# Low parts of the down-projection weights: a negated copy on ScalarE and an adding transfer instead of a subtraction on VectorE

## The chip, the cores and the metric

The kernel runs on one core of a Trainium2 chip. The metric is the device time of one execution in microseconds (us); of several runs the median is given.

## What is computed

A decoder trunk of two layers on an input of 512 tokens by 1024 columns in float32. Layer 0 mixes the tokens with gated linear recurrences, layer 1 with sparse attention. Each layer ends with a gated feed-forward block (FFN) with 2816 hidden columns, and that is the part that matters here:

```
def swiglu(h, w_gate_up, w_down):
    g, u = jnp.split(h @ w_gate_up, 2, axis=-1)
    return (jax.nn.silu(g) * u) @ w_down

h = h + swiglu(rmsnorm(h, ffn_norm[layer]), ffn_w_gate_up[layer], ffn_w_down[layer])
```

## The kernel before

Every matrix is used as a sum of two parts in the reduced format float32r: a high part (`wh` for weights) and a low part (`wl`, the weight minus its high part). A product of two such matrices is three matmuls: high by high, high by low, low by high (`mm3`, L86 to L90).

For a weight block, `load` (L58) has SP issue a transfer from memory into one of three buffers named `raw`. `split` (L70) then makes the two parts in pieces of 512 columns: ScalarE casts `raw` to `wh` (L77), VectorE subtracts `wh` from `raw` into `wl` (L78). `wh` and `wl` have seven buffers each. A `raw` buffer is free for the next load when all that read it is done.

The FFN (`ffn`, L270) goes over the hidden columns in 22 slices of 128, j = 0 to 21, in groups of 2, 4, 4, 4, 4, 4. In a slice:

- `weight_side` (L245) loads two blocks of gate and up weights of 512 KB each (L251), and makes from their quarters four sums on POOL (L259, L260, L262, L264). Each sum and three of the quarters are split into parts (`cut`, L208, and `split`). The sums let seven products stand for eight.
- Seven products (L290 to L299, called from L326 to L339) of 256 columns run on PE. ACT copies intermediate results (L327, L330, L335), VectorE adds (L331, L336, L338), POOL scales by the row norm (L341, L342), ACT applies the Silu (L343), VectorE multiplies (L344), and the result is split into `hh` (ACT, L347) and `hl` (VectorE, L348).
- From the second group on, each slice also multiplies two blocks of the second weight matrix with the hidden slices of the group before (`down`, L304 to L313, called at L352). Its weights come from `weight` (L66), 128x256 for the first group and 128x512 for the later ones.

After the last slice `down` runs once more in layer 0, for the eight blocks of the last group; in layer 1 `finish` (L363) does this instead, and gets its weights from `weight` as well.

The order of the instructions on each engine is set when the program is built, by a scheduler that works on the dependences; the engines then run their own lists in order. All transfers into `raw` are issued by SP, in order too.

Of the kernel before, what the change touches and what calls it, by code (L numbers as in the profile page):

```python
# [9 lines left out]
F32 = mybir.dt.float32  # L10
F32R = mybir.dt.float32r
U8 = mybir.dt.uint8
AF = mybir.ActivationFunctionType
ALU = mybir.AluOpType
# [3 lines left out]
P = 128  # L18
# [8 lines left out]
WS = 512  # L27
# [24 lines left out]
class Core:  # L52
# [17 lines left out]
    def split(self, raw, n, pool):  # L70
        nc = self.nc
        out = []
        for o in range(0, n, WS):
            m = min(WS, n - o)
            wh = self.wp.tile([P, WS], F32R, tag="wh", name="wh", bufs=7)
            wl = self.wp.tile([P, WS], F32R, tag="wl", name="wl", bufs=7)
            nc.scalar.copy(wh[:, :m], raw[:, o:o + m])  # L77
            (nc.gpsimd if pool else nc.vector).tensor_tensor(wl[:, :m], raw[:, o:o + m], wh.bitcast(F32)[:, :m],  # L78
                                                             ALU.subtract)
            out.append((wh, wl))  # L80
        return out

# [187 lines left out]
    def ffn(self, outs, w_out, gain, layer, next_gain):  # L270
        tc, nc, io, sp = self.tc, self.nc, self.io, self.sp
        with tc.tile_pool(name="fs", bufs=1) as fs, tc.tile_pool(name="fps", bufs=6, space=PSUM) as fps:
# [4 lines left out]
            for m in range(KD):  # L277
                ps = self.bank(self.turn + 1 + m // 3, "ps_o") if m in BANK_OUT else \
# [23 lines left out]
            out = []  # L302

            def down(hid, first, ms, last):  # L304

                nonlocal acc
                for m in ms:
                    ps = fps.tile([P, T], F32, tag="gu", name="ps_d") if last and m in OWN_DOWN else self.bank(m, "ps_d")
                    self.dense_t(ps, self.weight(io["dn"][layer, m, :, P * first:P * (first + len(hid))]), hid)
                    if last:  # L310
                        out.append(self.residual(m, ps, next_gain, acc))
                    else:
                        nc.vector.tensor_tensor(self.h[m], ps, self.h[m], ALU.add)  # L313


            before, first, done = None, 0, 0
            for size in GROUPS:
                hid = []
                for j in range(done, done + size):
# [30 lines left out]
                    if before:  # L350
                        n = KD // size
                        down(before, first, range((j - done) * n, (j - done + 1) * n), False)  # L352
                before, first = hid, done
                done += size
            tc.keep_in_program_order(nc.scalar.preload_act_table_set("natural_log_exp_and_others"))
            if next_gain is None:
                self.finish(hid, [io["dn"][layer, m, :, P * first:] for m in range(KD)], fps)
                return None, None
            acc = sp.tile([P, T], F32, tag="acc", name="acc", bufs=1)
            down(hid, first, range(KD), True)  # L360
            return out, acc

# [798 lines left out]
```

## Time and profile before

| | |
|---|---|
| median of 3 runs | 1341.58 us (1338.67 to 1341.74) |
| the profiled execution, its own time | 1340.35 us |
| its span, first to last instruction | 1338.2 us |
| mean granted TensorE clock | 0.98 |
| FFN of layer 0, POOL's first sum of the first and of the last slice | 272.3 and 602.3 us |
| FFN of layer 1, the same | 931.4 and 1261.5 us |

The profile is of one execution; its busy times are shares of the span. PE is TensorE, DVE VectorE, ACT ScalarE, POOL GpSimd, SP the engine that issues transfers (SPq its queue). A row of the timeline has the start, the duration, the engine and line, the operation with output and inputs, and in brackets how long the engine was idle before it and what released it.

### The profile page before, as it was taken

The page shows a single profiled execution, that of the slowest core. Times are in us where ns is not written, and L with a number is a line of the kernel's source. Part 1 is how long each engine was busy: PE and PEld are TensorE (multiplying, and loading weights), DVE is VectorE, ACT ScalarE, POOL GpSimd, SP SyncE. Part 2 cuts the span into 40 slices and gives each one's busy share as a digit, 9 for nine tenths or more (in the row PEclk, how much of TensorE's full clock was granted, in tenths as well). Part 3 has the DMA queues.
Part 4 walks back from the last instruction along what each step waited for, and adds up shares of the span by engine and source line. Part 5 has one row for each costly group of instructions (what it writes and reads, how often), then busy time and mean ns, then how long its engine had stood idle before and what let it go on. Part 6 is the DMA issues. An engine that isn't in the chain of part 4 may idle for free.

```text
span 1338.2 us, 21839 instructions
## 1 busy us (share of the span) xinstructions
PE 1276.7 (95%) x7846; PEld 1119.7 (84%) x7846; DVE 1016.4 (76%) x1829; ACT 729.4 (55%) x1587; POOL 643.9 (48%) x569
## 2 busy tenths in 40 slices
PE   9999999978999999999988999999799999999995
PEld 7888888868899888989876888877698999988883
DVE  7896764799999677775762888986989987766664
ACT  6655454655544444444554788995654444444444
POOL 3432430165666555553025666764665655555501
PEclk9999999999999999999998999999889999999997
DMA  7222211222233223332322211101123322223321
GB/s 254 84 74 69 79 49 63 79 83 79 84 103 110 95 96 99 107 102 89 104 86 94 72 56 48 48 9 63 51 84 124 98 96 95 95 95 96 103 63 63
DMA packets 44125, 115.13 MB, mean 86 GB/s; under 512 B 4913, under 2 KB 10481, under 8 KB 44017
## 3 DMA queue, kind: packets, MB, share of 16 engines
q1 hardware_dynamic: 43872, 113.69, 26.6%
q8 instruction: 62, 1.02, 0.3%
q14 instruction: 47, 0.38, 0.1%
q10 hardware_dynamic: 144, 0.04, 0.0%
HBM read 111.62 MB, written 2.10 MB: 85 GB/s over the span
## 4 chain that ended last, share of the span: by engine, by line
PE 54%; POOL 15%; DVE 15%; ACT 6%; DMA 6%; issue 5%; POOLq 0%; DVEq 0%; SPq 0%; ACTq 0%
DMA raw<-in_gu 5%; PE p L88 4%; PE p L89 4%; PE p L90 4%; PE ps_e L88 3%; PE ps_e L89 3%; PE ps_e L90 3%; DVE wl L78 3%; POOL sw L262 3%; POOL sw L264 3%; PE ps_d L90 3%; PE ps_d L89 3%; PE ps_d L88 3%; POOL sw L259 3%; POOL sw L260 2%
## 5 line engine op out<-in xcount | busy, mean ns | idle before, releaser
L78 DVE TENSOR_TENSOR wl<-raw,wh 128x512 fp32r<-128x512 f32 (+2 forms) x340 | 285.7, 846 | 51.1 <-ACT wh L77 50.4
L77 ACT CAST wh<-raw 128x512 fp32r<-128x512 f32 (+2 forms) x356 | 211.1, 604 | 179.9 <-PE p L89 44.9
L214 DVE TENSOR_TENSOR sl<-sw,sh 128x512 fp32r<-128x512 f32 x176 | 188.7, 1076 | 19.9 <-ACT sh L213 18.7
L259 POOL TENSOR_TENSOR sw<-raw 128x512 f32<-128x512 f32 x44 | 77.4, 1758 | 238.8 <-DMA raw<-in_gu 187.7
L213 ACT CAST sh<-sw 128x512 fp32r<-128x512 f32 x176 | 108.7, 617 | 118.0 <-PE p L89 80.9
L89 PE MATMUL ps_d<-hl,wh 128*128 128x512 f32 x344 | 136.1, 396 | 0.1
L90 PE MATMUL ps_d<-hh,wl 128*128 128x512 f32 x344 | 135.6, 394 | 0.0
L88 PE MATMUL ps_d<-hh,wh 128*128 128x512 f32 x344 | 135.0, 396 | 0.0
L343 ACT ACTIVATE g<-g 128x512 f32<-128x512 f32 x44 | 27.8, 632 | 135.7 <-POOL g L342 135.4
L344 DVE TENSOR_TENSOR g<-s,g 128x512 f32<-128x512 f32 x44 | 31.8, 722 | 72.1 <-ACT g L343 71.0
L927 POOL TENSOR_SCALAR p<-p,sm 128x128 f32<-128x128 f32 (+3 forms) x128 | 68.7, 557 | 32.5 <-DVE sm L924 11.9
L89 PE MATMUL ps_e<-xl,wh 128*128 128x512 f32 x192 | 76.8, 401 | 0.6 <-DVE xl L108 0.6
L88 PE MATMUL ps_e<-xh,wh 128*128 128x512 f32 x192 | 76.9, 404 | 0.2
L90 PEld LDWEIGHTS ps_d<-hh,wl 128*128 128x128 f32 x344 | 64.5, 188 | 14.8
L90 PE MATMUL ps_e<-xh,wl 128*128 128x512 f32 x192 | 76.5, 400 | 0.0
L918 ACT ACTIVATE p<-p,mx 128x256 f32<-128x256 f32 (+3 forms) x128 | 71.7, 565 | 8.8 <-DVE mx L910 8.3
L264 POOL TENSOR_TENSOR sw<-raw,sw 128x512 f32<-128x512 f32 x44 | 73.0, 1660 | 6.4 <-DVE sl L214 6.4
L89 PEld LDWEIGHTS ps_d<-hl,wh 128*128 128x128 f32 x344 | 64.7, 188 | 13.1 <-DVE hl L348 1.0
L88 PEld LDWEIGHTS ps_d<-hh,wh 128*128 128x128 f32 x344 | 64.5, 188 | 13.0
L262 POOL TENSOR_TENSOR sw<-raw 128x512 f32<-128x512 f32 x44 | 75.0, 1706 | 0.0
L342 POOL TENSOR_TENSOR g<-g,rstd 128x512 f32<-128x512 f32 x42 | 59.8, 1423 | 23.1 <-DVE g L338 23.1
L260 POOL TENSOR_TENSOR sw<-sw,raw 128x512 f32<-128x512 f32 x44 | 65.4, 1487 | 8.6 <-issue 4.8
(345 smaller groups left out, 4249.6 us busy)
## 6 DMA issues: line engine op xcount, KB each, us to landing
raw<-in_gu SPq DMA_DIRECT2D x88, 512.0 KB, 3.7
raw<-in_dn SPq DMA_DIRECT2D x80, 256.0 KB, 2.8
raw<-in_ein SPq DMA_DIRECT2D x22, 512.0 KB, 3.7
raw<-in_oin SPq DMA_DIRECT2D x12, 512.0 KB, 3.7
raw<-in_eout SPq DMA_DIRECT2D x8, 512.0 KB, 3.7
bias<-in_bias SPq DMA_DIRECT2D x16, 256.0 KB, 2.6
raw<-in_oout SPq DMA_DIRECT2D x8, 512.0 KB, 3.5
h<-in_x SPq DMA_DIRECT2D x8, 256.0 KB, 5.4
```

The costliest lines, as they stand in the source:

```text
L77: nc.scalar.copy(wh[:, :m], raw[:, o:o + m])
L78: (nc.gpsimd if pool else nc.vector).tensor_tensor(wl[:, :m], raw[:, o:o + m], wh.bitcast(F32)[:, :m], ALU.subtract)
L88: mm(ps, ah, bh, start=start, stop=False, skip_group_check=more)
L89: mm(ps, ah, bl, start=False, stop=False, skip_group_check=more)
L90: return mm(ps, al, bh, start=False, stop=stop, skip_group_check=more)
L213: nc.scalar.copy(hi, src)
L214: nc.vector.tensor_tensor(lo, src, hi.bitcast(F32), ALU.subtract)
L259: nc.gpsimd.tensor_tensor(s1, a21, a22, ALU.add)
L260: nc.gpsimd.tensor_tensor(s2, s1, a11, ALU.subtract)
L262: nc.gpsimd.tensor_tensor(s3, a11, a21, ALU.subtract)
L264: nc.gpsimd.tensor_tensor(s4, a12, s2, ALU.subtract)
L918: nc.scalar.activation(p, p, AF.Exp, bias=h["mx"][:, t, b:b + 1], scale=-1.0, accum_out=h["sm"][:, t, b:b + 1])
```

## The change

The weights of `down` come from a new method, `weight_add`, instead of `weight`. It casts as before, then ScalarE writes minus `wh` into `wl`, and a transfer issued by POOL adds `raw` onto `wl` inside SBUF. `finish` and all other weights keep `weight`.

```
@@ -77,6 +77,22 @@
+    def weight_add(self, ap):
+
+        nc = self.nc
+        n = ap.shape[1]
+        raw = self.load(ap)
+        out = []
+        for o in range(0, n, WS):
+            m = min(WS, n - o)
+            wh = self.wp.tile([P, WS], F32R, tag="wh", name="wh", bufs=7)
+            wl = self.wp.tile([P, WS], F32R, tag="wl", name="wl", bufs=7)
+            nc.scalar.copy(wh[:, :m], raw[:, o:o + m])
+            nc.scalar.activation(wl[:, :m], wh.bitcast(F32)[:, :m], AF.Identity, scale=-1.0)
+            nc.gpsimd.dma_start(wl.bitcast(F32)[:, :m], raw[:, o:o + m], accum_op=ALU.add)
+            out.append((wh, wl))
+        return out
...
@@ -306,7 +322,7 @@
-                    self.dense_t(ps, self.weight(io["dn"][layer, m, :, P * first:P * (first + len(hid))]), hid)
+                    self.dense_t(ps, self.weight_add(io["dn"][layer, m, :, P * first:P * (first + len(hid))]), hid)
```

Lines behind L81 stand 16 further down in the changed kernel: L259 becomes L275, L341 L357, L342 L358, L343 L359, L347 L363.

The order on the engines moves with it. On POOL, one slice in the late part of an FFN (the four sums, the scaling of `s` and of `g`). Before:

```order
L262 TENSOR_TENSOR sw<-raw 128x512
L341 TENSOR_TENSOR s<-s,rstd 128x256
L264 TENSOR_TENSOR sw<-raw,sw 128x512
L342 TENSOR_TENSOR g<-g,rstd 128x512
L259 TENSOR_TENSOR sw<-raw 128x512
L260 TENSOR_TENSOR sw<-sw,raw 128x512
```

And now:

```order
L278 TENSOR_TENSOR sw<-raw 128x512
L280 TENSOR_TENSOR sw<-raw,sw 128x512
L358 TENSOR_TENSOR g<-g,rstd 128x512
L95 DMA wl<-raw 128x512 x2
L275 TENSOR_TENSOR sw<-raw 128x512
L357 TENSOR_TENSOR s<-s,rstd 128x256
L276 TENSOR_TENSOR sw<-sw,raw 128x512
```

The two adds of a slice stand behind its last sum and the scaling of `g`, and ahead of the next slice's first sum.

On ACT, from the Silu of a slice to the casts of its two `dn` blocks. Before:

```order
L343 ACTIVATE g<-g 128x512
L213 CAST sh<-sw 128x512
L330 COPY u<-p_5607 128x256
L347 CAST hh<-g 128x512
L77 CAST wh<-raw 128x512 x2
L213 CAST sh<-sw 128x512
```

And now:

```order
L359 ACTIVATE g<-g 128x512
L93 CAST wh<-raw 128x512
L94 ACTIVATE wl<-wh 128x512
L363 CAST hh<-g 128x512
L93 CAST wh<-raw 128x512
L94 ACTIVATE wl<-wh 128x512
L229 CAST sh<-sw 128x512
```

The cast and the negation of the first block now stand directly behind the Silu, those of the second behind `hh`.

On SP, one slice of the changed kernel, with the semaphores that each issue waits for (DMAHW are those of SP's transfers, DMASW those of POOL's; 6 is the one that the add from `raw_5358` signals, 5 and 7 those of the second block's adds of the slice before and of this one):

```order
L63 DMA raw_5358<-in_dn 128x512 [waits DMAHW7_49,DMASW5_49,Activation_49]
L63 DMA raw_5379<-in_dn 128x512 [waits DMAHW0_49,DVE_49,Pool_49]
L267 DMA raw_5399<-in_gu 128x1024 [waits DMAHW1_49,DVE_49]
L267 DMA raw_5401<-in_gu 128x1024 [waits DMAHW2_49,DMASW6_49,Activation_49]
L63 DMA raw_5547<-in_dn 128x512 [waits DMAHW3_49,DMASW7_49,Activation_49]
```

The sequence of the loads is the one of before. The second gate/up block (`raw_5401`) waited for DVE there and now waits for the add from the first `dn` block.

## Rows read from the trace of the kernel before

**Rows 1.** The page: busy us, share of the span, instructions, by engine.

```profile
PE 1276.7 (95%) x7846; PEld 1119.7 (84%) x7846; DVE 1016.4 (76%) x1829; ACT 729.4 (55%) x1587; POOL 643.9 (48%) x569
```

**Rows 2.** Windows: length, busy PE, PEld, DVE, ACT, POOL, clock, DMA share, GB/s.

```profile
288.00:300.00 12.00, 4.79 (x35) 4.34 (x34) 12.00 (x20) 7.09 (x16) 5.96 (x4) 0.83 0.38 132
300.00:350.00 50.00, 45.99 (x339) 43.43 (x338) 48.38 (x69) 28.62 (x59) 31.54 (x19) 0.97 0.25 80
1099.98:1261.48 161.50, 159.48 (x1083) 144.90 (x1083) 115.89 (x171) 73.12 (x141) 86.92 (x61) 1.00 0.31 99
```

**Rows 3.** Timeline of POOL, one late slice in layer 1, next one's start.

```profile
1148.43 1.67 POOL L259 TENSOR_TENSOR sw<-raw 128x512 f32<-128x512 f32 x1 [7.29 <-DMA raw<-in_gu]
1150.18 1.30 POOL L260 TENSOR_TENSOR sw<-sw,raw 128x512 f32<-128x512 f32 x1
1151.43 1.75 POOL L262 TENSOR_TENSOR sw<-raw 128x512 f32<-128x512 f32 x1
1153.15 1.18 POOL L341 TENSOR_TENSOR s<-s,rstd 128x256 f32<-128x256 f32 x1
1154.30 1.73 POOL L264 TENSOR_TENSOR sw<-raw,sw 128x512 f32<-128x512 f32 x1
1155.99 1.29 POOL L342 TENSOR_TENSOR g<-g,rstd 128x512 f32<-128x512 f32 x1
1164.48 1.75 POOL L259 TENSOR_TENSOR sw<-raw 128x512 f32<-128x512 f32 x1 [7.21 <-DMA raw<-in_gu]
```

**Rows 4.** Timeline of ACT, the same slice.

```profile
1157.31 0.63 ACT L343 ACTIVATE g<-g 128x512 f32<-128x512 f32 x1 [4.76 <-POOL g L342]
1157.85 0.60 ACT L213 CAST sh<-sw 128x512 fp32r<-128x512 f32 x1
...
1158.70 0.62 ACT L347 CAST hh<-g 128x512 fp32r<-128x512 f32 x1
1159.23 1.14 ACT L77 CAST wh<-raw 128x512 fp32r<-128x512 f32 x2
```

**Rows 5.** Timeline of DVE, the same slice.

```profile
1159.52 0.68 DVE L348 TENSOR_TENSOR hl<-g,hh 128x512 fp32r<-128x512 f32 x1
1160.12 0.69 DVE L78 TENSOR_TENSOR wl<-raw,wh 128x512 fp32r<-128x512 f32 x1
```

**Rows 6.** Waits of SP's queue, 1148.43 to 1164.48: total us, times, longest.

```profile
SPq L251 <- DVE wl L78: 3.9, 1, 3.9
```

**Rows 7.** Issues of transfers, KB, median us to landing; then all `raw` loads.

```profile
raw<-in_gu SPq DMA_DIRECT2D x88, 512.0 KB, 3.7
raw<-in_dn SPq DMA_DIRECT2D x80, 256.0 KB, 2.8
...
raw<-in_dn SPq DMA_DIRECT2D x16, 128.0 KB, 2.2
...
DMA to landing us min/median/max: 2.0/3.6/6.4
```

**Rows 8.** Groups by form on POOL: busy us, mean ns, idle before.

```profile
L341 POOL TENSOR_TENSOR s<-s,rstd 128x256 f32<-128x256 f32 x44 | 49.5, 1126 | 35.2 <-DVE s L336 35.2
...
L927 POOL TENSOR_SCALAR p<-p,sm 128x128 f32<-128x128 f32 x32 | 13.2, 413 | 32.4 <-DVE sm L924 11.9 <-ACT ph L942 10.1 <-PE po L968 6.5
```

**Rows 9.** Timeline of POOL, first sum of slices 6 and 21, both layers.

```profile
363.79 2.27 POOL L259 TENSOR_TENSOR sw<-raw 128x512 f32<-128x512 f32 x1 [4.92 <-DVE hl L348]
...
602.34 1.40 POOL L259 TENSOR_TENSOR sw<-raw 128x512 f32<-128x512 f32 x1 [7.55 <-DMA raw<-in_gu]
...
1023.81 2.37 POOL L259 TENSOR_TENSOR sw<-raw 128x512 f32<-128x512 f32 x1 [4.81 <-ACT sh L213]
...
1261.48 1.73 POOL L259 TENSOR_TENSOR sw<-raw 128x512 f32<-128x512 f32 x1 [7.22 <-DMA raw<-in_gu]
```

**Rows 10.** Tile `ps_d`: the adds of layer 0's last eight blocks.

```profile
L201 DVE TENSOR_TENSOR h<-ps_d,h x8: 681/684/692, 645.3 to 661.6; 128x512 f32<-128x512 f32 x8
```

**Rows 11.** Timeline of DVE, a subtraction beside POOL's work.

```profile
1152.29 1.45 DVE L78 TENSOR_TENSOR wl<-raw,wh 128x512 fp32r<-128x512 f32 x1
```

## Prediction, on record before the changed kernel ran

> **What bounds the kernel now.** I read the page first: PE is busy 95% of the span, DVE 76%, ACT 55%, POOL 48% [rows 1]. Taken alone that says TensorE, and that relieving VectorE is worth little. The windows say where that holds. Late in the FFN of layer 1, over ten slices j (161.50 us), PE is busy 159.48 us and DVE only 115.89 [rows 2]; early in an FFN, from 300 to 350 us, it is DVE that is full (48.38 of 50) and PE that has room (45.99) [rows 2]. In the long late part the change therefore takes work from an engine that has 28% of its time free.
>
> The chain of waits, followed through one slice, shows a second bound in the same place. `raw` has three buffers for four loads a slice: two gate/up blocks (call them g0 and g1) and two blocks of the second product (d0 and d1). g1 gets the buffer that d0 leaves. In order of time: POOL starts its four sums when g1 lands, at 1148.43 us, and runs six instructions without a gap until 1155.99 + 1.29 = 1157.28 [rows 3]. ACT waits for that (4.76 us idle, released by POOL `g` L342), runs the Silu, then two smaller ones, `hh`, and the casts of d0 and d1, starting at 1159.23 [rows 4]. DVE writes d0's `wl` from 1160.12 to 1160.81 [rows 5]. That frees the buffer: SP's L251 load of g1 waits for DVE `wl` [rows 6], and POOL starts the next slice at 1164.48, 3.67 us later, named as waiting for `raw<-in_gu` [rows 3]. The circle is 8.85 (POOL) + 3.53 (ACT and DVE, 1157.28 to 1160.81) + 3.67 (load) = 16.05 us, with nothing idle in it: the slice's period. PE, with 2.0 us free in ten slices, has about the same length. What is put into this circle is paid in every slice; what is taken from DVE outside it is not seen.
>
> **The change part by part.** There are 96 loads of `dn` [rows 7]; eight belong to `finish`, which keeps `weight`. The other 88 blocks change: 72 of 256 KB, 16 of 128 KB.
>
> *Removed:* 88 subtractions on DVE. A full tile takes 0.69 us beside an idle POOL [rows 5] and up to 1.45 beside a busy one [rows 11]: some 60 to 90 us of DVE time. Only the 0.69 us of d0 lies in the circle.
>
> *Added on ACT:* 88 writes of minus the high part, 0.62 us each like the cast (0.60 to 0.63 for full tiles [rows 4]), 55 us in all. ACT has more than half its time free; d0's is in the circle, since the add cannot be issued before it.
>
> *Moved on ACT:* the order puts cast and negation of d0 right behind the Silu, ahead of `hh`. From POOL's end: 0.03 hop, 0.54 to the next start [rows 4], 0.62 cast, 0.62 negation, 0.05 hops: 1.9 us. This gives back what `hh` and two other instructions cost there before.
>
> *Added on POOL and the DMA engines:* the adds of d0 and d1 stand behind the last sum and behind `g`, and the next slice's first sum stands behind them. POOL waits there for g1 in any case, so d1's add, later by `hh` and another cast and negation, should be covered. If it weren't, its 2 us or so would come on top. SP's next load of d0 now waits for d1's add, a slice ahead of use. PE's first product with d0's `wl` stands in the following slice, so PE should meet the delay only through late g1 sums.
>
> *In the circle:* between the negation and the release stands the whole add, issue to landing. Call it A. The new circle is 3.67 + 8.85 + 1.9 + A = **14.4 + A**, against 16.05. It is longer as soon as A exceeds 1.7 us.
>
> A is in no row, since POOL issues no transfer in this trace. From below: the fastest landing of any `raw` load, 2.0 us; from above: the slowest, 6.4 [rows 7], plus the longest of POOL's own instructions in the slice, 1.75 [rows 3], together 8.2. I take the row that moves as much: the add of 256 KB reads two operands, 512 KB, and a 512 KB load lands 3.7 us after its issue [rows 7]. POOL has to set the transfer up; I estimate that at 0.8, between its shortest form (0.413) and its 128x256 product (1.126) [rows 8]. A = 4.5.
>
> For plain transfers from GpSimd the Trainium skill gives a price (DMA: Bandwidth & Descriptors, section Anatomy of one DMA): about 2.0 us and the bytes at 436 GB/s. That would be an estimate of 2.6 us for 256 KB and 1378 us by the sum below; no row here shows one, and it says nothing of an add's second read.
>
> *The sum.* The profiled execution took 1340.35 us (span 1338.2 and 2.1 around it), 1.2 under the median 1341.58. I count the 15 intervals per layer between POOL's seventh slice and its last: 363.79 to 602.34 and 1023.81 to 1261.48 [rows 9], 238.55 + 237.67 = 476.2 us. The slices before that I leave as they are: DVE fills them, gets shorter work, and the add stands earlier on POOL there. After: 30 x (14.4 + 4.5) = 567.0, so 90.8 more. Then the last eight blocks of layer 0, one every (661.6 - 645.3) / 7 = 2.33 us [rows 10]: with three buffers, each held for load 2.8, cast and negation 1.24 and add 4.5, one comes every 2.85, 4 us in all. 1340.35 + 90.8 + 4 = **1435 us**, or 1300 + 30 x A for other A: 1360 at 2.0, 1384 at 2.8 (the 256 KB load's own landing [rows 7]), 1492 at 6.4, 1546 at 8.2.
>
> **The rivals.** *Faster: the add is short and PE becomes the only bound.* Place: g1's load behind d0's add. It decides at A = 1.7. Below that the circle is shorter than PE's work and each slice can win only what PE idles, 0.2 us: 30 x 0.2 = 6, and up to 4 more per layer from the early DVE-bound slices (50 - 45.99). That is 1326. For it: DVE really is full there. Against it: no load of any size landed in under 2.0 us. Chance 0.04.
>
> *No difference.* A near 1.7, or g1's buffer freed some other way than by the add; the order of waits on SP speaks against it. Within 4 us of 1340: 0.03.
>
> *The add is no dearer than a fast load,* A of 2.0 to 2.65: POOL's issue costs next to nothing, and the second read is hidden. 1360 to 1380, chance 0.05.
>
> *POOL is held up while it sets the transfer up.* DVE's instructions take up to 1.45 us beside POOL's against 0.69 alone [rows 5, 11], so the two already hinder each other. Two such waits before the transfer starts add 2.9: A = 7.4, 1522 us. For it: the same rows; against it: ahead of d0's add POOL is idle in the trace, and DVE's work there shrinks. Chance 0.09. The Trainium skill has a rule that speaks against the change in this way (SBUF — State Buffer, section SBUF: two separate sides): descriptors of GpSimd's transfers are not written while DVE holds the shared port in its two-port modes. By that rule's own list `tensor_tensor` has no such mode, so it would not bite here; no run here shows it yet.
>
> *PE's clock falls in the new pauses.* From 288 to 300 us PE was busy 4.79 of 12 us and the granted clock was 0.83 [rows 2]. The new pause is near 2.8 us a slice. PE at the lower level for 3 us of work takes 3 longer, about what the slice has spare, so I put no price on it alone.
>
> **How the numbers follow.** Forecast, A from 2.65 to 7.2: 0.79, 1380 to 1515 us. The dear add, 0.09, lies above; the fast add, 0.05, below; no difference 0.03; faster 0.04. So faster 0.04, same 0.03, slower 0.93, where 0.3% (4 us) is about what a measurement of this kernel can tell. The range 1380 to 1515 leaves out some 2 in 10, both ends set by A.
>
> **What would show it.** In the late slices POOL's first sums should stand 18 to 20 us apart, still released by `raw<-in_gu`; SP's load of g1 should wait for the add's landing, where it waited for DVE `wl`; from the negation's end to that load should be A. PE should show one pause of 2 to 4 us per slice. DVE's busy time should fall by 60 to 90 us and ACT's rise by 55. If the intervals are longer but SP's g1 load waits for POOL or ACT, the circle is right and its dear term is not the transfer. If PE waits directly for `wl`, the adds came a slice later than I read from the order. If the intervals stay near 16, A is under 2 or g1 is not behind it, and the forecast is wrong.

## The result, and the profile after

| | us |
|---|---|
| before, median of the runs beside the changed kernel | 1341.66 (1338.67 to 1342.65) |
| changed kernel, median of 4 runs | 1406.74 (1404.45 to 1411.84) |
| ratio | 1.0494, 95% interval 1.0461 to 1.0527 |
| predicted | 1435, range 1380 to 1515, slower with a chance of 0.93 |
| the profiled execution of the changed kernel, and its span | 1411.84, 1409.9 |

The change costs 65 us by the medians and 71.7 us between the two profiled spans (1338.2 and 1409.9); the profiled execution of the changed kernel was the longest of its four. The direction and the range held; the predicted time was 28 us too high. The sections below work with the spans, since durations come from them.

The page of the changed kernel, busy us by engine, against [rows 1]:

```profile
PE 1302.2 (92%) x7846; PEld 1141.8 (81%) x7846; DVE 1012.4 (72%) x1741; ACT 773.4 (55%) x1675; POOL 685.6 (49%) x657
```

ACT has 44 us more, for the 88 negations (forecast: 55). POOL has 41.7 us more. What is new there is a group of its own on the page, the issues of the adds (busy us, mean ns of one, then idle time before them). They alone make 76.7 us, so POOL's arithmetic, the same instructions as before, takes less time now:

```profile
L95 POOL DMA_DIRECT2D wl<-raw x88 | 76.7, 872 | 123.3 <-ACT wl L94 119.6
```

DVE lost 88 instructions and only 4 us of busy time, which is taken up below. The transfers, KB each and median us from issue to landing, against [rows 7]:

```profile
raw<-in_gu SPq DMA_DIRECT2D x88, 512.0 KB, 3.8
raw<-in_dn SPq DMA_DIRECT2D x80, 256.0 KB, 2.8
wl<-raw POOLq DMA_DIRECT2D x72, 256.0 KB, 3.4
```

The loads land within 0.1 us of before. The add of 256 KB inside SBUF takes 3.4 us, longer than a load of 256 KB from memory.

Now one late slice of layer 1, the view that [rows 3] showed of before. POOL's timeline (start, duration, engine and line, operation; in brackets the idle time before it and what ended it):

```profile
1190.63 1.28 POOL L275 TENSOR_TENSOR sw<-raw 128x512 f32<-128x512 f32 x1 [4.54 <-DMA raw<-in_gu]
1191.89 0.73 POOL L357 TENSOR_TENSOR s<-s,rstd 128x256 f32<-128x256 f32 x1
1192.58 1.29 POOL L276 TENSOR_TENSOR sw<-sw,raw 128x512 f32<-128x512 f32 x1
1193.84 1.74 POOL L278 TENSOR_TENSOR sw<-raw 128x512 f32<-128x512 f32 x1
1195.54 1.74 POOL L280 TENSOR_TENSOR sw<-raw,sw 128x512 f32<-128x512 f32 x1
1197.23 1.74 POOL L358 TENSOR_TENSOR g<-g,rstd 128x512 f32<-128x512 f32 x1
1201.11 0.87 POOL L95 DMA_DIRECT2D wl<-raw  x1 [2.14 <-ACT wl L94]
1202.80 0.86 POOL L95 DMA_DIRECT2D wl<-raw  x1 [0.82 <-ACT wl L94]
1208.02 1.28 POOL L275 TENSOR_TENSOR sw<-raw 128x512 f32<-128x512 f32 x1 [4.36 <-DMA raw<-in_gu]
```

ACT's negation of d0 in it, SP's timeline over the same piece, SP's wait from 1190.63 to 1208.02 us (total us, times, longest), and its waits from 1150 to 1330 us, against [rows 6]:

```profile
1200.18 0.63 ACT L94 ACTIVATE wl<-wh 128x512 fp32r<-128x512 f32 x1
```

```profile
1197.72 7.03 SPq L267 DMA_DIRECT2D raw<-in_gu  x2
```

```profile
SPq L267 <- DMA wl<-raw: 6.3, 1, 6.3
```

```profile
SPq L267 <- DMA wl<-raw: 58.9, 10, 6.9
SPq L63 <- POOL sw L280: 57.3, 7, 8.9
SPq L63 <- DMA wl<-raw: 38.8, 10, 8.7
```

The circle of the prediction can be read off. POOL works from 1190.63 to 1198.97, 8.34 us. Then 2.14 us pass until the first add (d0's) is issued at 1201.11: Silu, cast and negation on ACT. SP's pair of gate/up loads stands in its queue from 1197.72 and ends at 1197.72 + 7.03 = 1204.75; its last 0.33 is the second load's own issue (the length of a single issue in the same answer), so g1 goes out at 1204.42, 3.31 us after d0's add was issued. SP's wait names the releaser: the landing of `wl<-raw`. The load lands and POOL starts the next slice at 1208.02, 3.60 later. 8.34 + 2.14 + 3.31 + 3.60 = 17.39, the whole distance from 1190.63 to 1208.02, against 16.05 before. d1's add, at 1202.80, lies inside POOL's wait for g1, as predicted.

The four first sums that frame the 15 intervals of each layer, against [rows 9]:

```profile
369.31 1.29 POOL L275 TENSOR_TENSOR sw<-raw 128x512 f32<-128x512 f32 x1 [4.19 <-DMA raw<-in_gu]
...
636.72 1.29 POOL L275 TENSOR_TENSOR sw<-raw 128x512 f32<-128x512 f32 x1 [4.52 <-DMA raw<-in_gu]
...
1066.73 1.28 POOL L275 TENSOR_TENSOR sw<-raw 128x512 f32<-128x512 f32 x1 [3.88 <-DMA raw<-in_gu]
...
1333.98 1.29 POOL L275 TENSOR_TENSOR sw<-raw 128x512 f32<-128x512 f32 x1 [4.68 <-DMA raw<-in_gu]
```

267.41 + 267.25 = 534.7 us instead of 476.2: 58.5 of the 71.7. The slices ahead of these (from the first sum of slice 0 at 271.6 and 966.3) take 97.7 and 100.4 where they took 91.5 and 92.4: 14.2. What is left, -1.0, lies before the first FFN (-0.7) and behind the last slices (+0.5 and -0.8).

### The profile page after: what moved, and what is told of

It is laid out like the page before. It is cut to its first block, busy times and chain, and to the rows that moved or that the text cites. A ratio compares the mean times of both kernels' runs of the same rounds, so it can differ in the third digit from the quotient of the medians.

```text
span 1409.9 us, 22005 instructions
## 1 busy us (share of the span) xinstructions
PE 1302.2 (92%) x7846; PEld 1141.8 (81%) x7846; DVE 1012.4 (72%) x1741; ACT 773.4 (55%) x1675; POOL 685.6 (49%) x657
## 4 chain that ended last, share of the span: by engine, by line
PE 50%; POOL 11%; DVE 10%; ACT 10%; issue 9%; DMA 9%; ACTq 0%; SPq 0%; DVEq 0%; POOLq 0%
DMA raw<-in_gu 6%; PE p L104 4%; PE p L105 4%; PE p L106 3%; PE ps_e L104 3%; PE ps_e L105 3%; PE ps_e L106 3%; POOL g L358 3%; DVE wl L78 2%; PE ps_d L104 2%; POOL sw L280 2%; PE ps_d L105 2%; PE ps_d L106 2%; POOL sw L275 2%; PE po L982 2%
## 5 line engine op out<-in xcount | busy, mean ns | idle before, releaser
L230 DVE TENSOR_TENSOR sl<-sw,sh 128x512 fp32r<-128x512 f32 x176 | 218.2, 1255 | 138.5 <-ACT sh L229 128.3
L78 DVE TENSOR_TENSOR wl<-raw,wh 128x512 fp32r<-128x512 f32 (+1 forms) x252 | 237.9, 956 | 54.1 <-ACT wh L77 53.6
L77 ACT CAST wh<-raw 128x512 fp32r<-128x512 f32 (+1 forms) x268 | 160.4, 612 | 111.1 <-PE ps_o L105 22.8
L275 POOL TENSOR_TENSOR sw<-raw 128x512 f32<-128x512 f32 x44 | 58.8, 1337 | 196.6 <-DMA raw<-in_gu 189.6
L95 POOL DMA_DIRECT2D wl<-raw x88 | 76.7, 872 | 123.3 <-ACT wl L94 119.6
L104 PE MATMUL p<-t4h,wh 128*128 128x256 f32 x176 | 54.7, 311 | 32.1 <-ACT u L351 32.0
L934 ACT ACTIVATE p<-p,mx 128x256 f32<-128x256 f32 (+3 forms) x128 | 71.7, 565 | 10.2 <-DVE mx L926 9.7
L278 POOL TENSOR_TENSOR sw<-raw 128x512 f32<-128x512 f32 x44 | 75.2, 1708 | 3.8 <-DVE sl L230 3.8
L93 ACT CAST wh<-raw 128x512 fp32r<-128x512 f32 (+1 forms) x88 | 50.7, 576 | 46.4 <-DMA raw<-in_dn 25.6
L358 POOL TENSOR_TENSOR g<-g,rstd 128x512 f32<-128x512 f32 x42 | 69.7, 1660 | 9.2 <-DVE g L354 9.2
```

Of the source, the lines that this page charges most:

```text
L95: nc.gpsimd.dma_start(wl.bitcast(F32)[:, :m], raw[:, o:o + m], accum_op=ALU.add)
L104: mm(ps, ah, bh, start=start, stop=False, skip_group_check=more)
L230: nc.vector.tensor_tensor(lo, src, hi.bitcast(F32), ALU.subtract)
L275: nc.gpsimd.tensor_tensor(s1, a21, a22, ALU.add)
L278: nc.gpsimd.tensor_tensor(s3, a11, a21, ALU.subtract)
L358: (nc.vector if j == NF - 1 else nc.gpsimd).tensor_tensor(g, g, r, ALU.mult)
```

## The experiments

The theory, called circle below, is that of the prediction: d0's add stands between the negation and the load of g1, and each late slice is longer by it. The sums over the 30 late intervals are made as above. The kernel before took 1340.86 us beside the first four runs, 1343.51 beside the next four, 1341.36 beside the last one; each ratio is to it. In e4, e5 and e9 the first slice of an FFN also starts earlier (by 4.6 us in layer 0 of e4), which their early column doesn't show.

| run | us | ratio, 95% interval | 30 late intervals | early slices, both layers |
|---|---|---|---|---|
| before, [rows 9] for its late intervals | 1340.35 (profiled) | | 476.2 | 183.9 |
| changed kernel | 1406.74 | 1.0494 (1.0461 to 1.0527) | 534.7 | 198.1 |
| e1, only d0 by the add | 1390.07 | 1.0368 (1.0348 to 1.0388) | 520.4 | 193.2 |
| e2, only d1 by the add | 1340.32 | 0.9994 (0.9985 to 1.0004) | 480.3 | 184.0 |
| e3, VectorE adds | 1348.67 | 1.0058 (1.0042 to 1.0074) | 483.4 | 186.8 |
| e4, adds with four `raw` buffers | 1337.53 | 0.9975 (0.9965 to 0.9985) | 466.4 | 193.2 |
| e5, before with four `raw` buffers | 1336.41 | 0.9949 (0.9937 to 0.9962) | 462.8 | 194.8 |
| e6, plain copy from POOL | 1372.56 | 1.0219 (1.0205 to 1.0233) | 504.0 | 193.9 |
| e7, plain copy from ScalarE | 1350.89 | 1.0062 (1.0048 to 1.0076) | 490.1 | 190.2 |
| e8, adds for the first group only | 1349.73 | 1.0051 (1.0038 to 1.0065) | 472.3 | 197.5 |
| e9, four buffers, only d1 by the add | 1335.36 | 0.9962 (0.9948 to 0.9977) | 462.1 | 193.8 |

**e1 and e2: which of the two adds costs.** Of the two blocks of a slice, even `m` is d0, odd `m` is d1.

```
-    self.dense_t(ps, self.weight_add(io["dn"]...
+    self.dense_t(ps, (self.weight if m % 2 else self.weight_add)(io["dn"]...
```

> Only the first of a slice's two dn blocks (d0) keeps the negation and the adding transfer; the second (d1) goes back to the subtraction on VectorE. Theory circle (d0's add stands between POOL's last instruction of a slice and the load of g1, and its 3.3 us are paid per slice): nearly the whole loss stays, 1390 to 1412 us, late slices 17.3 to 18 us apart. Rival issue (POOL spends 0.87 us on each issue and waits for the negations, ACT has 0.62 us more per block; each block costs its share): half the loss, 1365 to 1382 us. Rival traffic (the adds' bytes slow the loads from memory): half the loss as well.

e2 has the two names exchanged.

> The other half: only d1 keeps the negation and the adding transfer, d0 is subtracted on VectorE. Theory circle: d1's buffer goes to the next d0, not to g1, so the loss is nearly gone, 1335 to 1352 us, late slices 16.0 to 16.4 us apart. Rivals issue and traffic: half the loss, 1365 to 1382 us.

d0's add alone brings most of the loss, 1390.07; d1's add alone nothing, although it moves as many bytes, takes as long on POOL (879 ns an issue, 878 in e1) and lands even later (median 3.8 against 3.3). The two differ in one respect that the circle cares about: who waits. In e1 the late slices stand 17.3 us apart on average, in e2 16.0. e1 came out at the lower edge of what was expected, because the two effects don't add up: 49 and -1 against 65 us. Between the profiles of e1 and of the changed kernel lie 14.3 us in the late intervals and 4.9 in the early slices, so d1's add costs something where d0's is there too; this is taken up, in part, behind e7.

**e3: the same detour over ScalarE, without a transfer.** ScalarE writes the negated high part, VectorE adds.

```
-    nc.gpsimd.dma_start(wl.bitcast(F32)[:, :m], raw[:, o:o + m], accum_op=ALU.add)
+    nc.vector.tensor_tensor(wl[:, :m], raw[:, o:o + m], wl.bitcast(F32)[:, :m], ALU.add)
```

> All 88 blocks keep ScalarE's negation, but VectorE adds raw onto it instead of a transfer. Theory circle: only 0.65 us of ACT come into the circle, and the order puts hh ahead of the casts again; 0.65 x 30 = 20 us at most, 1341 to 1365 us. Rival ACT (the 55 us that the negations add on ACT are what is paid): 1390 us or more.

1348.67: the negation in the circle costs 0.58%, or 7.8 us. The other 58 of the 65 us come with the transfer.

**e4 and e5: one buffer more.** A fourth `raw` buffer (`bufs=3` to 4, paid by one `tr` buffer, 7 to 6), so that g1's load needn't wait for d0's add; e5 does the same to the kernel before.

> The changed kernel with a fourth raw buffer (and one buffer fewer of the small tr tiles, to make room). g1 then waits for a gate/up block of the slice before and not for the add. Theory circle: the loss is gone though all 88 adds, issues and negations are there, 1330 to 1352 us, late slices 15.8 to 16.3 us apart, PE without pauses. Rivals issue, traffic and ACT: 1385 us or more, since their work is all still there.

> The kernel before (subtraction on VectorE) with a fourth raw buffer and one tr buffer fewer: the control for the changed kernel with a fourth buffer, which ran in 1337.5. Theory circle: the fourth buffer opens the loop through g1's load, whatever makes the low part; the kernel before was only just bound by that loop, so it gains little too: 1332 to 1340, and the late slices stand 16.0 to 16.2 apart, set by PE. Rival: the gain of 0.25% came from VectorE's shorter list, then this run stays within 0.1% of the kernel before, 1340 to 1343, and the adds with four buffers are worth 3 to 4 us.

With the fourth buffer the adds cost little: 1337.53 instead of 1406.74, with all 88 adds in place. Windows from 1100 to 1260 us (columns as in [rows 2]), first e4, then e5:

```profile
1100.00:1260.00 160.00, 159.84 (x1102) 148.11 (x1102) 124.64 (x154) 87.20 (x163) 93.30 (x83) 1.00 0.52 135
```

```profile
1100.00:1260.00 160.00, 160.00 (x1103) 148.48 (x1102) 123.12 (x174) 75.74 (x143) 80.99 (x63) 1.00 0.32 101
```

PE is busy all but 0.16 us in e4 and throughout in e5. The late intervals are 466.4 and 462.8 us, both under the 476.2 of before, and the early slices longer than there; early and late together make 659.6 and 657.6 us, against 660.1 before and 732.8 in the changed kernel. On average the late slices stand 15.5 and 15.4 us apart, closer than either expectation said. That locates the loss in the loop through the buffers; SP in e4 (1100 to 1260 us) waits longest for the adds with the loads of `dn`, a slice ahead of use:

```profile
SPq L63 <- DMA wl<-raw: 115.1, 18, 8.9
SPq L267 <- DVE wl L78: 16.7, 10, 2.0
```

The control corrects a first reading of e4: its 0.25% against the kernel before is not a gain of the adds, since the buffer alone gains 0.51%. Beside that control the adds cost some 0.26%, 3.5 us, and the two intervals don't overlap. With the loop open the adds relieve nobody who is waited for.

**e6 and e7: what in the add takes 3.4 us.** Both leave out the subtraction: the low part then holds the whole weight. e6 drops the accumulation, e7 also lets ScalarE issue the copy.

```
-    nc.gpsimd.dma_start(wl.bitcast(F32)[:, :m], raw[:, o:o + m], accum_op=ALU.add)
+    nc.gpsimd.dma_start(wl.bitcast(F32)[:, :m], raw[:, o:o + m])
```

> The transfer from POOL copies raw over wl instead of adding it (the subtraction is left out; the low part then holds the whole weight). One operand is read instead of two, all else in place. Theory circle with the set-up as the price: the landing time falls little, from 3.4 to 2.6 to 3.2 us, and the time to 1407 - 30 x (0.2 to 0.8) = 1383 to 1401. Rival, the accumulation is the price: the landing falls to the 2.0 to 2.2 of the fastest loads, and the time to 1365 to 1371. A landing of 3.3 to 3.5 and a time within 5 us of 1407 would say that the second operand costs nothing.

> The same plain copy (the subtraction is left out), issued by ScalarE instead of POOL. The order of the program moves with it: POOL loses the two issues per slice, ScalarE's casts stand behind one more operation. Theory circle with POOL's set-up as part of the price: the landing is 2.0 to 2.8 us, as for loads from memory, the circle 8.3 + 2.1 + 2.4 + 3.6 = 16.4 to 17 us, and the time 1350 to 1370. Rival, the move of data itself is the price, whoever issues it: the landing stays at 3.2 to 3.4, the time at 1385 to 1407.

e6 went against what I expected of the circle theory, and near its rival: 1372.56 us, 34 us under the changed kernel. The landings, of e6 and then of e7:

```profile
wl<-raw POOLq DMA_DIRECT2D x72, 256.0 KB, 2.4
```

```profile
wl<-raw ACTq DMA_DIRECT2D x72, 256.0 KB, 2.5
```

Accumulating costs 1.0 us per transfer: 3.4 against 2.4, same engine, same bytes written. The pages' rows of POOL's queue, changed kernel and e6, say where most of it lies (packets, MB, their time as a share of sixteen DMA engines' span):

```profile
q0 software_dynamic: 12672, 20.98, 9.1%
```

```profile
q0 software_dynamic: 6528, 20.98, 4.1%
```

By the spans of 1409.9 and 1371.6 us that is 128 and 56 us, or 1.5 and 0.6 us for each of the 88 transfers. The issue on POOL also shrinks, from 872 to 565 ns, by the rows of L95 on the pages:

```profile
L95 POOL DMA_DIRECT2D wl<-raw x88 | 49.7, 565 | 117.8 <-ACT wl L94 114.1
```

And the circle turns that 1.0 us into time as predicted: 30 x 1.0 = 30, measured 534.7 - 504.0 = 30.7 in the late intervals. The slope of the forecast is confirmed, with a split of the add's price that the forecast didn't have.

Who issues the copy matters little for the landing (2.5 from ScalarE). e7 is another 14 us faster in the late intervals for a reason of order: in 12 of the 30 POOL's L357 stands ahead of the first sum, in the wait for g1, and is out of the chain. These 12 take 15.8 us on average, the other 18 take 16.7, about as long as e6's 16.8. One such slice, POOL's timeline in e7:

```profile
1241.53 0.74 POOL L357 TENSOR_TENSOR s<-s,rstd 128x256 f32<-128x256 f32 x1 [6.08 <-DVE s L352]
1243.78 1.29 POOL L275 TENSOR_TENSOR sw<-raw 128x512 f32<-128x512 f32 x1 [1.50 <-DMA raw<-in_gu]
...
1249.81 1.73 POOL L358 TENSOR_TENSOR g<-g,rstd 128x512 f32<-128x512 f32 x1
1259.48 1.30 POOL L275 TENSOR_TENSOR sw<-raw 128x512 f32<-128x512 f32 x1 [7.94 <-DMA raw<-in_gu]
```

POOL's part is 7.76 us there instead of 8.34, and the slice 15.70. So e7 doesn't isolate the issuing engine; its landing does.

**The slices with an add in POOL's chain.** In six of the 30 late intervals of the changed kernel d1's add stands behind L357, within POOL's run. They take 18.4 to 18.8 us; the other 24 average 17.6. I first thought that what happens to DVE there (last section) is the price. e6 speaks against it: its slices with the copy at that place are longer too, 17.6 to 18.3 us against 16.4 to 17.0 (from the fourth interval of a layer on), and nothing of the kind happens to DVE there. The trace of the changed kernel has the chain of one of the six, from 1172.24 to 1190.63. SP's wait from 1171 to 1181 us, its loads of `dn` and of gate/up, ACT's cast of d0 and the issue of d0's add:

```profile
SPq L63 <- DMA wl<-raw: 8.7, 1, 8.7
```

```profile
1177.51 3.54 SPq L63 DMA_DIRECT2D raw<-in_dn  x2
1181.14 5.28 SPq L267 DMA_DIRECT2D raw<-in_gu  x2
```

```profile
1180.34 0.62 ACT L93 CAST wh<-raw 128x512 fp32r<-128x512 f32 x1 [0.82 <-DMA raw<-in_dn]
```

```profile
1181.92 0.88 POOL L95 DMA_DIRECT2D wl<-raw  x1 [1.82 <-ACT wl L94]
```

d1's add of the slice before is issued only at 1174.18. The load of the new d0 waits for it and goes out at 1177.51, ACT casts d0 at 1180.34, d0's add is issued at 1181.92, and g1 goes out at 1186.09 (1181.14 + 5.28 - 0.33). 1.94 + 3.33 + 2.83 + 1.58 + 4.17 + 4.54 = 18.39, the whole slice: here both adds lie in the chain, one after the other. In e6's slice from 1142.95 the cast does not wait; there d0's copy is late, landing 4.5 us after its issue where the next slice's takes 2.3. No run takes this place by itself, and it is not the main part of what d1's add costs beside d0's: against the same intervals of e1 the six are 3.1 us longer of 14.3, while 9.4 lie in the first four intervals of the two layers. Why those are longer, no run shows.

**e8: the early slices.** The forecast left them unchanged; the trace has 14.2 us. Only the first group's `dn` blocks (128x256, 16 in both layers together) keep the add:

```
-    self.dense_t(ps, self.weight_add(io["dn"]...
+    self.dense_t(ps, (self.weight if first else self.weight_add)(io["dn"]...
```

> Only the weights of the first group (16 blocks of 128x256 per layer's four slices, j 2 to 5) come by the add; the later 72 blocks of 128x512 keep the subtraction. Theory: about 12 of the 65 us that the change costs arise in these early slices (the seventh slice began 5.5 us later in layer 0, 8.0 in layer 1), so 1346 to 1355 here, with the late slices 16 us apart as before. Rival: the early delay came from the 128x512 blocks that are loaded ahead for the next group, then this run stays at 1340 to 1343.

1349.73 us, 6.2 above the kernel before; the early slices take 13.6 us more than in before, almost all of the changed kernel's 14.2, and the late ones 3.9 less. So these 16 small adds are the cause, not the larger ones loaded ahead. Waits of SP in e8 from 300 to 366 us:

```profile
SPq L267 <- DMA wl<-raw: 12.7, 4, 4.5
```

It is the same loop: g1 behind an add. In the trace of before the largest wait of that kind in the window was 2.2 us, for DVE, and three of POOL's first sums were already released by a load:

```profile
SPq L251 <- DVE wl L78: 3.3, 2, 2.2
```

```profile
318.45 1.30 POOL L259 TENSOR_TENSOR sw<-raw 128x512 f32<-128x512 f32 x1 [2.11 <-DMA raw<-in_gu]
...
334.43 1.61 POOL L259 TENSOR_TENSOR sw<-raw 128x512 f32<-128x512 f32 x1 [1.54 <-DMA raw<-in_gu]
...
348.31 1.79 POOL L259 TENSOR_TENSOR sw<-raw 128x512 f32<-128x512 f32 x1 [2.64 <-DMA raw<-in_gu]
```

So the loads were late there already, beside the full DVE.

**e9: a version that combines both.** Four buffers, and d1 alone by the add.

> A fourth raw buffer (one tr buffer fewer), and only the second block of each slice by the add; the first keeps the subtraction. Theory circle: neither the fourth buffer's loop nor the second block's add bounds a slice, so the time is that of the kernel before with four buffers, 1335 to 1339 (0.3 to 0.6% under the kernel before), late slices 15.4 to 15.6 us apart, as there. Rival: half the adds take work from VectorE where it is full, early in each FFN, then this run comes below 1333.

1335.36 us, ratio 0.9962 (0.9948 to 0.9977), against 0.9949 (0.9937 to 0.9962) for the buffer alone: within each other's intervals. Both beat both kernels; the gain is the buffer's, and half the adds bring nothing on top.

## Why the prediction was right, and what it mis-sized

*The bound and the place were right.* The circle g1, POOL, ACT, d0's release was predicted to bound the late slices, and the add to be paid in each. SP's L267 waits for `wl<-raw`, POOL's first sum for `raw<-in_gu`, and d0's add alone (e1) or the loop opened (e4) moves the time as that says.

*The size of A was too high.* I took 4.5: 3.7 for the landing of a load of 512 KB and 0.8 for POOL's setting up. The late slice shows 3.31 from issue to release with the set-up in it, and the median landing is 3.4. Counted as the forecast defined A, from the negation's end (1200.18 + 0.63 = 1200.81) to the load of g1, it is 3.61. Two readings went into the miss. An add reads 512 KB but behaved as a 256 KB copy of 2.4 plus 1.0 for accumulating, not as a load of 512 KB; and the set-up is not on top: the 3.31 us, counted from the start of POOL's 0.87, hold it. The other terms nearly held: POOL 8.34 for 8.85 (the first sum took 1.28 where it took 1.67 [rows 3]; L357's 0.73 for 1.18 and L358's 1.74 for 1.29 cancel), ACT 1.84 to the negation's end for 1.9, the load 3.60 for 3.67. Together 17.39 where 18.9 was forecast; averaged over all 30 intervals, with the longer ones, 534.7 / 30 = 17.8.

For a transfer from GpSimd the Trainium skill's price (DMA: Bandwidth & Descriptors, section Anatomy of one DMA) gave an estimate of 2.6 us for 256 KB. The runs agree for the plain copy (2.4) and not for the adding one (3.4).

*The early slices were not free.* "The slices before that I leave as they are: DVE fills them" was the step that failed: +14.2 us. A full DVE in a window (48.38 of 50 [rows 2]) doesn't say that no load is waited for inside it. This miss and that of the late intervals (534.7 for 567.0, 32.3 us too much forecast) partly cancelled, so the total is nearer to the forecast than its terms are. *The tail* of layer 0 was forecast at +4 and came out at +0.5. *d1's add* was to be covered by POOL's wait for g1. So it is where it stands alone (e2), but beside d0's add it brings 14.3 us in the late intervals (e1 against the changed kernel), most of it unexplained.

*VectorE's relief was smaller than written.* DVE's busy time was to fall by 60 to 90 us and fell by 4. The page's groups of the changed kernel:

```profile
L230 DVE TENSOR_TENSOR sl<-sw,sh 128x512 fp32r<-128x512 f32 x176 | 218.2, 1255 | 138.5 <-ACT sh L229 128.3
L78 DVE TENSOR_TENSOR wl<-raw,wh 128x512 fp32r<-128x512 f32 (+1 forms) x252 | 237.9, 956 | 54.1 <-ACT wh L77 53.6
```

The same two groups of before, from its page:

```profile
L78 DVE TENSOR_TENSOR wl<-raw,wh 128x512 fp32r<-128x512 f32 (+2 forms) x340 | 285.7, 846 | 51.1 <-ACT wh L77 50.4
L214 DVE TENSOR_TENSOR sl<-sw,sh 128x512 fp32r<-128x512 f32 x176 | 188.7, 1076 | 19.9 <-ACT sh L213 18.7
```

The subtractions lost 47.8 us (285.7 - 237.9). But the parts of the sums took 29.5 more (L214, now L230, 1076 to 1255 ns each), and the mean of an L78 rose from 846 to 956 ns. That is what more meetings with POOL's instructions would do [rows 5, 11]; no run tried it by itself, and the rest of the gap, 14.3 us, was not traced.

*The rivals.* None came in. No fast add (A of 2.0 to 2.65): that is the plain copy of e6. No hold-up of POOL's transfer of the size that was priced (A = 7.4): from issue to landing no add of the changed kernel took over 6.1 us, and the median is 3.3. Some landings are late, 21 of the 88 adds over 4 us, but so are 10 of the 88 copies that ScalarE issues in e7. The Trainium skill's rule on descriptors that wait for DVE (SBUF — State Buffer, section SBUF: two separate sides) does not show in this, as its own list of modes has it. *The pauses of PE* came about once per slice, but shorter than the 2 to 4 us of the forecast. PE's waits over the late intervals of layer 1, 1066.73 to 1333.98 us (total us, times, longest):

```profile
PE p L104 <- ACT u L351: 11.5, 8, 2.0
PE ps_d L104 <- ACT hh L363: 8.5, 3, 3.1
PE p L104 <- ACT u L346: 1.8, 2, 1.3
```

With layer 0's that is 26 waits of 43.0 us in the 30 intervals, 1.7 on average, and none directly for an add. Over the late window 1166 to 1328 us the granted clock is 0.98, where it was 1.00 [rows 2]. PE's busy time in the 30 intervals grew with it, from 470.9 to 490.2 us for about as many matmuls (3222 and 3238 in the traces), and 44.5 us of the 534.7 are left as idle time. So PE had room for the lower clock; no run prices it by itself.

## What to carry to other kernels

Before work is moved from one engine to another, look at what the moved step releases: here the last reader of a load buffer stood in a loop with no slack, and a step of 0.69 us was replaced by 0.6 of negation and 3.3 of transfer, once per slice. A transfer that only its consumer waits for can be slow at little or no cost (e2, e4); one that a buffer waits for is paid in full, and a further buffer is the cheaper cure (e5 gains 0.5% by itself). And a window in which one engine is full may still hold waits for loads: look at the releasers of single instructions before a term is set to zero.

## What the runs showed of the hardware

An adding transfer inside SBUF of 256 KB landed 3.4 us after its issue by POOL, a copying one 2.4; the issue kept POOL busy for 0.87 and 0.57 us.

In six places of the changed kernel POOL goes straight on to four instructions of arithmetic after issuing an add, and in each of them an instruction of VectorE that starts beside them ends only behind POOL's last. POOL's timeline in one of them, then DVE's:

```profile
1174.18 0.86 POOL L95 DMA_DIRECT2D wl<-raw  x1
1174.79 1.58 POOL L276 TENSOR_TENSOR sw<-sw,raw 128x512 f32<-128x512 f32 x1
...
1178.53 1.57 POOL L280 TENSOR_TENSOR sw<-raw,sw 128x512 f32<-128x512 f32 x1
```

```profile
1175.15 5.51 DVE L78 TENSOR_TENSOR wl<-raw,wh 128x512 fp32r<-128x512 f32 x1
```

POOL's three sums and a scaling start 1.24 to 1.26 us apart there, where the same four stand 1.26 to 1.70 apart in the slice from 1190.63, and a subtraction that takes 0.69 us beside an idle POOL takes 5.51, until POOL is done. There are six such rows in the changed kernel (5.48 to 5.51 us); single instructions of DVE of over 3.4 us are ten in e2, twelve in e4 and two in e9, none in before, e1, e3, e5, e6, e7 or e8. e6 has the copy at the same six places, and DVE's L78 beside it took:

```profile
1213.97 1.49 DVE L78 TENSOR_TENSOR wl<-raw,wh 128x512 fp32r<-128x512 f32 x1
```

So it was seen only with the accumulating form, issued ahead of several of POOL's own instructions (in e1 and e8 at most one follows an add at once). Why, no run shows. It cost little here: e2 has ten of them and no loss.
